# Moving the preparation of attention biases to an earlier stage, and their loads to another DMA queue

## The chip, the cores and the metric

One core of a Trainium2 chip runs the whole program: two transformer blocks, one after the other, in one launch. The metric is device time in microseconds (us), lower is better, for one execution; three executions of the kernel before are at hand, and one further execution was recorded by the hardware profiler.

## The reference, cut to what matters

The first block has two layers, A and B, the second has two more. Each layer is a mixer (attention) and then a feed-forward part. What the change touches is the second layer's attention over a grid of 8 rows and 64 columns of tokens, which adds a learned bias for every relative position, and the keys and values of 256 memory tokens, which each of the two layers attends to as well:

```python
def first_block(x, mem, ...):
    mem_n = rmsnorm(mem, norm_mem)
    for i in range(DEPTH):                       # DEPTH = 2: layer A, layer B
        h = rmsnorm(x, norm_mix[i])
        mkv = mem_n @ w_mem_kv[i]                # keys and values of the 256 memory tokens
        if i % 2 == 0:
            q, k, v, qm = split(h @ w_in_a[li])
            y_tok = windowed_gqa(q, k, v, sink_a[li])
        else:
            q, k, v, qm = split(h @ w_in_b[li])
            y_tok = neighbourhood_attn(q, k, v, rpb_b[li])
        y_mem = memory_attn(qm, mk, mv)
        x = x + concat([y_tok, y_mem]) @ w_out[i]
        h = rmsnorm(x, norm_ffn[i])
        gu = h @ w_gate_up[i]                    # 1024 -> 2 * 2816
        x = x + (silu(gu[..., :D_FF]) * gu[..., D_FF:]) @ w_down[i]

def neighbourhood_attn(q, k, v, rpb):            # rpb: 12 heads x 15 x 31
    bias = rpb[:, dr_idx][:, :, :, dc_idx]       # row and column offset of query and key
    s = einsum(q, k) * D ** -0.5 + bias
    ...
```

## The kernel before, in words

**Arithmetic.** Every float32 product is made of three matmuls: a number is split into a high part `hi` (ScalarE, ACT, L429) and the rest `lo` (VectorE, DVE, L430), and `mm3` (L254 to L256; `linN`, L283 to L285, with the operands the other way round) adds hi by hi, hi by lo and lo by hi in PSUM. A weight piece (`wpiece`) is a 128x4x256 tile: one DMA on SyncE's queue (SP, L213) into one of four `raw` buffers, then the split into one of four `hi` and `lo` buffers. From the fifth feature tile of a feed-forward part on, `seven` (loads at L304) and `blocks_to` make a larger product of seven block products, with additions by DVE and ACT around them.

**Layer A's attention (about 30 to 200 us).** The pairs of heads pass through four-step units: scores (`qk`, L847 and L848), softmax (DVE L721, then exp on ACT, L723), transposes of the probabilities on TensorE (PE, `tr`, L1166) and their copy out of PSUM by ACT (L1168), and the product with the values (`pv`, L1177). Between these units a list of generators, `fill` (L1183), is stepped, so that PE has other work while the softmax runs: query tiles, then `memory_kv()`, then the last query tiles `q_tiles([20, 21, 22, 23])`, then the output projection. `memory_kv` makes keys and values of the memory tokens for both layers: the keys are copied out of PSUM (L872), split and copied to the other half of the partitions (`stack_k`: ACT L834, DVE L835, GpSimd (POOL) L840 and L841), the values are copied out at L880. Layer A's are used at once; layer B's go to a DRAM tile `memd` by five DMAs on SP (L886).

**Layer A's feed-forward part (254 to 573 us).** `ffn` runs 22 tiles f of 128 features, in groups of four (one of two); each tile ends with `put`, whose product at L1043 occurs once for each f. The down projection of one group is spread over the next group's tiles. The same function runs layer B's feed-forward part (831 to 1142 us).

**The biases.** `load_biases` is a generator that `ffn` steps with `next(mid)` at the start of each tile from f = 4 on (L999; `MID = 4`), in layer A alone. It clears a DRAM tile `rpbs` (memset on POOL, one DMA), writes the table into it by eight DMAs on POOL's queue (L1220), spreads it into a second DRAM tile `TBd` by 16 DMAs on SP (L1224; each moves 768 pieces of 128 bytes), and then loads `TBd` into six SBUF tiles `TB` (L1230) and, by `memory_back`, `memd` into five tiles `memb` (L897), all on SP. In layer B, POOL makes the masked biases out of `TB` (L1334 and following), and PE reads `memb` in the memory attention.

**What sets the order.** The program is written through a scheduler: it takes the instructions in the order in which the generators make them, with what each waits for, and by its own model of durations lays down one order for each engine and each queue; the chip then executes every engine's list in that order, and waits for semaphores where something isn't ready. So a generator's place in `fill` is a wish, and what an engine really executes is its list.

## Time and profile before

| what | value |
|---|---|
| time, three executions | 2470.08, 2470.57 (median), 2476.79 us |
| profiled execution: its own time | 2472.3 us |
| profiled execution: span | 2470.6 us |
| mean granted clock of PE, share of full | 0.995 |
| PE busy | 2428.9 us (98%) |
| DVE, ACT, POOL busy | 1812.7, 1185.9, 232.4 us |
| layer A's feed-forward part, first to last L1043 | 254.2 to 572.6 us |
| layer B's feed-forward part, first to last L1043 | 831.4 to 1142.1 us |

The span is what the profiler saw from the first to the last instruction; the execution's own time is 1.7 us longer and is the one to hold against the three times. PE is busy nearly all the time, so a change in time shows as PE idle time that comes or goes, or as a stretch in which PE's granted clock (PEclk, in shares of 2.4 GHz) is lower. A busy time on another engine matters only where PE waits for it.

### The profile page before, as it was taken

What the parts mean: (1) busy time and instruction counts of PE and PEld (TensorE: products, weight loads), DVE (VectorE), ACT (ScalarE), POOL (GpSimd) and SP (SyncE); (2) the same over time, 40 slices, a digit from 0 to 9 for tenths busy, and PEclk for the clock granted to TensorE, in tenths of its full rate; (3) what the DMA queues carried; (4) which work ended last, traced back from release to release, by engine and by line L of the source; (5) the groups of instructions that cost most, each with busy time, mean ns of one, the idle gap of its engine ahead of it and who ended that gap; (6) DMA issues with size and microseconds to landing.
All of it is one profiled execution on the core that took longest, in us unless ns stands there. A gap on an engine that the chain in (4) does not pass through costs nothing.

```text
span 2470.6 us, 44131 instructions
## 1 busy us (share of the span) xinstructions
PE 2428.9 (98%) x17446; PEld 2195.4 (89%) x17446; DVE 1812.7 (73%) x3531; ACT 1185.9 (48%) x2175; POOL 232.4 (9%) x359
## 2 busy tenths in 40 slices
PE   7999999999999999999999999999999999999999
PEld 6787789998887889998989999899999988989998
DVE  6875767777775778777766656888886775788885
ACT  4764435444565445445432233445444664445543
POOL 3120300003130100001011110200000000200000
PEclk9999999999999999999999999999999999999999
DMA  6152234444222223333411123123334222223332
GB/s 189 52 141 82 77 83 113 116 145 145 86 74 78 77 86 107 103 102 101 130 44 52 35 83 91 56 86 107 98 95 142 58 57 75 69 83 109 99 98 82
DMA packets 345443, 229.17 MB, mean 93 GB/s; under 512 B 54435, under 2 KB 335444, under 8 KB 345236
## 3 DMA queue, kind: packets, MB, share of 16 engines
q1 hardware_dynamic: 342212, 217.55, 30.0%
q0 software_dynamic: 2864, 8.77, 1.2%
q8 instruction: 137, 2.24, 0.4%
q14 instruction: 70, 0.57, 0.1%
q10 hardware_dynamic: 160, 0.04, 0.0%
HBM read 214.10 MB, written 13.74 MB: 92 GB/s over the span
## 4 chain that ended last, share of the span: by engine, by line
PE 83%; DVE 10%; issue 3%; ACT 2%; POOL 1%; SPq 1%; DMA 1%; DVEq 0%; ACTq 0%; POOLq 0%
PE mm L254 19%; PE mm L256 19%; PE mm L255 19%; PE pss L254 3%; PE pss L256 3%; PE pss L255 3%; DVE lo L430 2%; PE pso L254 1%; PE pso L256 1%; PE pso L255 1%; PE pss L847 1%; DVE xb L430 1%; PE pso L808 1%; PE pss L848 1%; PE pso L2045 1%
## 5 line engine op out<-in xcount | busy, mean ns | idle before, releaser
L429 ACT ACTIVATE hi<-raw 128x1024 fp32r<-128x1024 f32 (+1 forms) x454 | 470.7, 1039 | 520.5 <-PE pss L255 245.5
L430 DVE TENSOR_TENSOR lo<-raw,hi 128x1024 fp32r<-128x1024 f32 (+1 forms) x454 | 550.6, 1215 | 131.7 <-ACT hi L429 130.8
L254 PE MATMUL mm<-xh,hi 128*128 128x264 f32 (+3 forms) x1256 | 413.2, 329 | 8.0 <-ACT xh L508 2.4
L255 PE MATMUL mm<-xl,hi 128*128 128x264 f32 (+3 forms) x1256 | 405.3, 323 | 1.3 <-DVE xl L509 1.2
L256 PE MATMUL mm<-xh,lo 128*128 128x264 f32 (+3 forms) x1256 | 404.6, 323 | 0.0
L254 PE MATMUL mm<-ah,hi 128*128 128x512 f32 (+1 forms) x880 | 308.8, 352 | 7.5 <-DVE ut L404 4.9
L256 PE MATMUL mm<-xb,lo 128*128 128x256 f32 (+2 forms) x1088 | 308.1, 283 | 4.2 <-DVE lo L430 4.2
L255 PE MATMUL mm<-al,hi 128*128 128x512 f32 (+1 forms) x880 | 307.9, 350 | 0.1
L256 PE MATMUL mm<-ah,lo 128*128 128x512 f32 (+1 forms) x880 | 307.7, 350 | 0.0
L254 PE MATMUL mm<-xb,hi 128*128 128x256 f32 (+2 forms) x1088 | 307.3, 282 | 0.0
L255 PE MATMUL mm<-xb,hi 128*128 128x256 f32 (+2 forms) x1088 | 306.9, 282 | 0.0
L254 PEld LDWEIGHTS mm<-xh,hi 128*128 128x128 f32 x1256 | 238.8, 190 | 32.7 <-issue 6.7
L255 PEld LDWEIGHTS mm<-xl,hi 128*128 128x128 f32 x1256 | 238.9, 190 | 18.6 <-DVE xl L509 2.7
L256 PEld LDWEIGHTS mm<-xh,lo 128*128 128x128 f32 x1256 | 238.4, 190 | 18.4 <-issue 0.5
L687 DVE TENSOR_TENSOR xr<-mm,xr 128x512 f32<-128x512 f32 (+1 forms) x288 | 158.1, 558 | 124.1 <-PE mm L256 123.9
L256 PEld LDWEIGHTS mm<-xb,lo 128*128 128x128 f32 x1088 | 205.6, 189 | 5.1 <-DVE lo L430 5.0
L254 PEld LDWEIGHTS mm<-xb,hi 128*128 128x128 f32 x1088 | 205.5, 189 | 3.1 <-ACT hi L429 0.7
L255 PEld LDWEIGHTS mm<-xb,hi 128*128 128x128 f32 x1088 | 205.5, 189 | 2.2
L254 PEld LDWEIGHTS mm<-ah,hi 128*128 128x128 f32 x880 | 165.5, 188 | 29.8 <-DVE ut L404 6.6
L256 PEld LDWEIGHTS mm<-ah,lo 128*128 128x128 f32 x880 | 165.5, 188 | 22.7
L255 PEld LDWEIGHTS mm<-al,hi 128*128 128x128 f32 x880 | 165.5, 188 | 18.9 <-DVE al L430 1.1
L254 PE MATMUL pss<-xb,hi 128*128 128x256 f32 (+2 forms) x544 | 154.6, 284 | 0.0
(526 smaller groups left out, 5041.4 us busy)
## 6 DMA issues: line engine op xcount, KB each, us to landing
raw<-in_w_gate_up_dram SPq DMA_DIRECT2D x142, 256.0 KB, 3.0
raw<-in_ffn_w_up_dram SPq DMA_DIRECT2D x142, 256.0 KB, 3.0
raw<-in_w_down_dram SPq DMA_DIRECT2D x40, 512.0 KB, 3.4
raw<-in_ffn_w_down_dram SPq DMA_DIRECT2D x40, 512.0 KB, 3.4
raw<-in_mix_w_in_dram SPq DMA_DIRECT2D x28, 512.0 KB, 3.8
raw<-in_w_in_b_dram SPq DMA_DIRECT2D x20, 512.0 KB, 3.8
a<-in_w_gate_up_dram SPq DMA_DIRECT2D x34, 256.0 KB, 3.4
a<-in_ffn_w_up_dram SPq DMA_DIRECT2D x34, 256.0 KB, 2.9
```

The costliest lines, as they stand in the source:

```text
L254: PE.matmul(ps, r32(hi), r32(xh), start=first, stop=False, skip_group_check=more)
L255: PE.matmul(ps, r32(hi), r32(xl), start=False, stop=False, skip_group_check=more)
L256: PE.matmul(ps, r32(lo), r32(xh), start=False, stop=last, skip_group_check=more)
L429: A.activation(r32(dst_h), src, AF.Copy)
L430: V.tensor_tensor(r32(dst_l), src, dst_h, ALU.subtract)
L687: V.tensor_tensor(X[j][:, o:o + n], ps[:, :n], X[j][:, o:o + n], ALU.add)
L808: PE.matmul(po[64 * hh:64 * hh + 64, b * P:(b + 1) * P], self.vals(b, j, h), pt[:, (2 * hh + j) * P:(2 * hh + j + 1) * P], start=j == 0, s ...
L847: PE.matmul(ps[:, :n], r32(q), r32(k[0][:, k0:k0 + n]), start=True, stop=False)
L848: PE.matmul(ps[:, :n], r32(q), r32(k[1][:, k0:k0 + n]), start=False, stop=True)
L2045: PE.matmul(po[64 * hh:64 * hh + 64, b * P:(b + 1) * P], vt[b + j][:, kv * 64:kv * 64 + 64], PT[:, (2 * hh + j) * P:(2 * hh + j + 1) * P], ...
```

## The change

The generator `load_biases` is cut in three. `biases_out` (memset, and the nine DMAs on POOL's queue that fill `rpbs`) becomes the first generator of layer A's `fill`. `biases_columns` (the 16 DMAs `TBd<-rpbs`, on SP as before) is called twice there: columns 0 to 7 ahead of `memory_kv()`, columns 8 to 15 behind it and ahead of the last query tiles. `biases_back` (the six loads `TB<-TBd` and the five loads `memb<-memd`) is called once, ahead of the last group's down projection in layer A's `ffn`, and issues on POOL's queue instead of SP's. `ffn` no longer steps a generator per tile. No operation is added or removed otherwise.

```diff
--- before.py
+++ after.py
@@ -890,11 +890,11 @@
             memK.append(kst)
             memV.append(vt)
 
-    def memory_back():
+    def memory_back(eng):
         d = memK[1]
         t = [slot("memb") for _ in range(5)]
         for i, x in enumerate(t):
-            nc.sync.dma_start(x[:, :512], d[i * P:(i + 1) * P, :])
+            eng.dma_start(x[:, :512], d[i * P:(i + 1) * P, :])
         memK[1] = [[(t[2 * i + hh][:, :256], t[2 * i + hh][:, 256:512]) for hh in range(2)] for i in range(2)]
         memV[1] = [t[4][:, :256], t[4][:, 256:512]]
 
@@ -979,7 +979,8 @@
             o = max(lo, d)
             V.scalar_tensor_tensor(out[:, o:T], src[:, o - d:T - d], taps[n - 1 - d], out[:, o:T], ALU.mult, ALU.add)
 
-    def ffn(X, T, nj, wgu, wd, taps, done, lo=0, mid=None):
+    def ffn(X, T, nj, wgu, wd, taps, done, mid=None, lo=0):
+
 
         xs = nj.xs
         lg = max(0, lo - 2)
@@ -996,8 +997,6 @@
 
         def up(f, put, between):
             c = f * P
-            if mid is not None and f >= MID:
-                next(mid, None)
             gt, ut = wk("gt"), wk("ut")
             if f < NPLAIN:
                 pcs = [wcols(wgu, 4 * h, [(c, P), (DFF + c, P)]) for h in range(2)]
@@ -1055,6 +1054,8 @@
                 up(f0 + i, put, more)
                 more(8)
             before = down(gi, acts)
+        if mid is not None:
+            mid()
         run(before)
 
     def dump(X, T, off=0):
@@ -1078,6 +1079,31 @@
     mnat = load_rows_of(a["mem"][0], NMEM)
 
 
+    TB, rel = [], {}
+
+    def scap(off, dims):
+        return bass.AP(tensor=rel["sc"].tensor, offset=rel["sc"].offset + off, ap=dims)
+
+    def biases_out():
+
+        rel["sc"] = dp.tile([P, 288], F32, name="rpbs")
+        z = slot("zpad")[:, :288]
+        G.memset(z, 0.0)
+        G.dma_start(rel["sc"], z)
+        for r in range(8):
+            G.dma_start(scap(r * 4608 + 8, [[384, 12], [48, 8], [1, 31]]), a["rpb_b"][0, :, 7 - r:15 - r, :])
+        yield 0.1
+
+    def biases_columns(lo, hi):
+
+        if lo == 0:
+            rel["td"] = dp.tile([P, 6 * 512], F32, name="TBd")
+        for cc in range(lo, hi):
+            nc.sync.dma_start(rel["td"][8 * cc:8 * cc + 8, :].rearrange("p (i j) -> p i j", j=32),
+                              scap(15 - cc, [[4608, 8], [48, 96], [1, 32]]))
+        yield 0.1
+
+
     def layer_a(X):
         w = a["w_in_a"][0]
         sk = cp.tile([P, 24], F32, name="sinkA")
@@ -1180,8 +1206,8 @@
 
         order = [0, 1, 3, 4, 2, 5, 6, 7]
         heads = A_PAIRS + [(12, 13), (14, 15)]
-        fill = Fill(q_tiles([6, 9, 7, 10], [3, 4]), q_tiles([2, 5, 8, 11], [2, 5]), memory_kv(),
-                    q_tiles([20, 21, 22, 23], [6, 7]))
+        fill = Fill(biases_out(), q_tiles([6, 9, 7, 10], [3, 4]), q_tiles([2, 5, 8, 11], [2, 5]),
+                    biases_columns(0, 8), memory_kv(), biases_columns(8, 16), q_tiles([20, 21, 22, 23], [6, 7]))
         wo = a["w_out"][0]
         return mixer(lambda p: PairA(p) if p < 6 else MemPair(0, p - 6, qt[p]), order,
                      lambda p: fill.until(lambda: p in qt and (p < 6 or len(memV) == 2)), fill,
@@ -1204,35 +1230,15 @@
                         X[j][:, :S].rearrange("p (r c) -> p r c", c=64), ALU.add)
         lag.put(XB[j])
 
-    TB = []
-
-    def load_biases():
-
-        sc = dp.tile([P, 288], F32, name="rpbs")
-        z = slot("zpad")[:, :288]
-        G.memset(z, 0.0)
-        G.dma_start(sc, z)
-
-        def scap(off, dims):
-            return bass.AP(tensor=sc.tensor, offset=sc.offset + off, ap=dims)
-
-        for r in range(8):
-            G.dma_start(scap(r * 4608 + 8, [[384, 12], [48, 8], [1, 31]]), a["rpb_b"][0, :, 7 - r:15 - r, :])
-
-        td = dp.tile([P, 6 * 512], F32, name="TBd")
-        for cc in range(16):
-            nc.sync.dma_start(td[8 * cc:8 * cc + 8, :].rearrange("p (i j) -> p i j", j=32),
-                              scap(15 - cc, [[4608, 8], [48, 96], [1, 32]]))
-            if cc > 1:
-                yield
+    def biases_back():
         for hp in range(6):
             TB.append(slot("TB"))
-            nc.sync.dma_start(TB[hp][:, :512], td[:, hp * 512:(hp + 1) * 512])
-        memory_back()
+            G.dma_start(TB[hp][:, :512], rel["td"][:, hp * 512:(hp + 1) * 512])
+        memory_back(G)
 
     nb = Norm(S, ("norm_mix", 1), "rsB")
     lag = Lag(nb, NLAG)
-    ffn(X, S, nf, a["w_gate_up"][0], a["w_down"][0], None, to_cols, mid=load_biases())
+    ffn(X, S, nf, a["w_gate_up"][0], a["w_down"][0], None, to_cols, biases_back)
     lag.end()
     if stop == "a":
         return dump(XB, S)
@@ -1863,7 +1869,7 @@
     def ffn2(X, li, done, lo=0):
         fw = load_rows([([("f", li, j) for j in range(3)],
                          a["ffn_conv_w_2"][li].rearrange("j (c p) -> (j c) p", p=P), NFF)], f"fwcol{li}")
-        ffn(X, T, nf, a["ffn_w_up_2"][li], a["ffn_w_down_2"][li], lambda f: tap(fw, ("f", li), 3, f), done, lo)
+        ffn(X, T, nf, a["ffn_w_up_2"][li], a["ffn_w_down_2"][li], lambda f: tap(fw, ("f", li), 3, f), done, None, lo)
 
     def to_norm(j, out):
         resid(X)(j, out)
@@ -2173,7 +2179,6 @@
 LATER = (0, 3)
 ABQ = 16
 POOLSQ = (1, 3, 5, 7)
-MID = 4
 MSTEP = 2
 RATIO_A = 0.7
 RATIO_B = 1.2
```

The three places where this changes an engine's list, as the scheduler laid it down (names with a number are buffers; x4 means four like instructions; line numbers are those of the kernel that the fence is of).

SP's queue in layer A's attention, the kernel before: the last two loads for the memory keys and values, the two loads of the last query weights (`raw<-in_w_in_a`), loads of the output weights, and the first store to `memd`.

```order
L213 DMA raw_1740<-in_w_mem_kv_dram 128x4x256
L213 DMA raw_1746<-in_w_mem_kv_dram 128x4x256
L213 DMA raw_1810<-in_w_in_a_dram 128x4x256
L213 DMA raw_1816<-in_w_in_a_dram 128x4x256
L213 DMA raw_2009<-in_w_out_dram 64x2x256 x4
L213 DMA raw_2164<-in_w_out_dram 64x256 x2
L213 DMA raw_2164<-in_w_out_dram 64x2x256
L213 DMA raw_2164<-in_w_out_dram 64x256
L213 DMA raw_2164<-in_w_out_dram 64x3x256
L213 DMA raw_2363<-in_w_out_dram 64x2x256
L886 DMA memd<-memk_1694 128x512
L213 DMA raw_2363<-in_w_out_dram 64x2x256 x2
```

The same place in the changed kernel:

```order
L213 DMA raw_1761<-in_w_mem_kv_dram 128x4x256
L213 DMA raw_1767<-in_w_mem_kv_dram 128x4x256
L1102 DMA TBd<-rpbs 768x32
L886 DMA memd<-memk_1715 128x512
L886 DMA memd<-memk_1716 128x512
L886 DMA memd<-memk_1751 128x512
L886 DMA memd<-memk_1752 128x512
L886 DMA memd<-memv_1676 128x512
L1102 DMA TBd<-rpbs 768x32 x7
L213 DMA raw_1839<-in_w_in_a_dram 128x4x256
L213 DMA raw_1845<-in_w_in_a_dram 128x4x256
L213 DMA raw_2038<-in_w_out_dram 64x2x256 x4
```

The two loads of query weights stood ahead of all five stores to `memd`; now they stand behind them, and behind eight `TBd<-rpbs` DMAs (one ahead of the stores, seven behind).

PE in layer A's attention, the kernel before, within the memory keys of layer B (L254 to L256 with `xm` are the keys' matmuls, L847 and L848 attention scores):

```order
L254 MATMUL mm_1704<-xm_1251,hi_1658 128x256
L255 MATMUL mm_1704<-xm_1251,hi_1658 128x256
L847 MATMUL pss_1573<-kh_362,qs_1136 128x384
L848 MATMUL pss_1573<-kl_363,qs_1136 128x384
L256 MATMUL mm_1704<-xm_1251,lo_1659 128x256
L254 MATMUL mm_1704<-xm_1261,hi_1664 128x256
L255 MATMUL mm_1704<-xm_1261,hi_1664 128x256
L256 MATMUL mm_1704<-xm_1261,lo_1665 128x256
L254 MATMUL mm_1704<-xm_1272,hi_1664 128x256
L255 MATMUL mm_1704<-xm_1272,hi_1664 128x256
```

The changed kernel, just ahead of those keys (L1203 is `pv`, L1192 the transposes `tr`); behind these rows come 48 matmuls for layer B's keys, 48 for its values and 48 for the last two query tiles, with no attention row between them:

```order
L1203 MATMUL pso_1989<-PT_1894,vA_233 64x128
L1192 MATMUL pss_1934<-ident,Pa_1370 128x128 x3
L1203 MATMUL pso_1989<-PT_1901,vA_233 64x128
L1203 MATMUL pso_1989<-PT_1894,vA_234 64x128
L1203 MATMUL pso_1989<-PT_1901,vA_234 64x128
L1203 MATMUL pso_1989<-PT_1894,vA_235 64x128
L1203 MATMUL pso_1989<-PT_1901,vA_235 64x128
L1192 MATMUL pss_1941<-ident,Pa_1376 128x128 x3
L1203 MATMUL pso_1989<-PT_1938,vA_234 64x128
L1203 MATMUL pso_1989<-PT_1945,vA_234 64x128
L1203 MATMUL pso_1989<-PT_1938,vA_235 64x128
L1203 MATMUL pso_1989<-PT_1945,vA_235 64x128
```

The attention steps that were spread among the keys' and values' matmuls now stand together ahead of them, one unit's transposes close behind another's products.

SP's queue in layer A's feed-forward part at f = 4 to 6, the kernel before (L304 and L213 load weights):

```order
L304 DMA raw_3417<-in_w_gate_up_dram 128x4x128
L304 DMA raw_3415<-in_w_gate_up_dram 128x4x128
L1224 DMA TBd<-rpbs 768x32 x5
L304 DMA raw_3416<-in_w_gate_up_dram 128x4x128
L213 DMA raw_3514<-in_w_down_dram 128x2x256
L1224 DMA TBd<-rpbs 768x32
L304 DMA raw_3573<-in_w_gate_up_dram 128x4x128
L304 DMA raw_3571<-in_w_gate_up_dram 128x4x128
L304 DMA raw_3572<-in_w_gate_up_dram 128x4x128
L213 DMA raw_3670<-in_w_down_dram 128x2x256
```

The changed kernel at the same place:

```order
L304 DMA raw_3428<-in_w_gate_up_dram 128x4x128
L304 DMA raw_3426<-in_w_gate_up_dram 128x4x128
L304 DMA a_3739<-in_w_gate_up_dram 128x4x128
L304 DMA raw_3427<-in_w_gate_up_dram 128x4x128
L213 DMA raw_3525<-in_w_down_dram 128x2x256
L304 DMA raw_3583<-in_w_gate_up_dram 128x4x128
L304 DMA raw_3581<-in_w_gate_up_dram 128x4x128
L304 DMA raw_3582<-in_w_gate_up_dram 128x4x128
L304 DMA a_3894<-in_w_gate_up_dram 128x4x128
```

The list now holds weight loads alone. The eleven loads of `TB` and `memb`, which stood in it at f = 18, are in POOL's list behind that part's last arithmetic on POOL. The lists of PE, DVE and ACT for layer A's feed-forward part are now row for row those of layer B's.

## Rows read from the trace of the kernel before

**Rows 1.** The page: the span, then busy us, share and count of each engine.

```profile
span 2470.6 us, 44131 instructions
...
PE 2428.9 (98%) x17446; PEld 2195.4 (89%) x17446; DVE 1812.7 (73%) x3531; ACT 1185.9 (48%) x2175; POOL 232.4 (9%) x359
```

**Rows 2.** Line L1043, 240 to 600 us: count, ns min/median/max, first and last start.

```profile
L1043 DVE TENSOR_TENSOR ut<-ut,gt x22: 683/685/693, 254.2 to 572.6; 128x512 f32<-128x512 f32 x22
```

**Rows 3.** The same view, 700 to 1300 us: the feed-forward part of layer B.

```profile
L1043 DVE TENSOR_TENSOR ut<-ut,gt x22: 676/684/718, 831.4 to 1142.1; 128x512 f32<-128x512 f32 x22
```

**Rows 4.** Windows: busy us (xcount) of PE, PEld, DVE, ACT, POOL; PEclk, DMA share.

```profile
340.00:345.00 5.00, 3.09 (x16) 2.07 (x15) 4.20 (x8) 3.33 (x6) 0.00 (x0) 1.00 0.00 0
346.70:350.20 3.50, 3.50 (x19) 3.50 (x18) 1.90 (x3) 1.00 (x2) 0.00 (x0) 0.51 0.85 235
885.00:1000.00 115.00, 115.00 (x822) 107.55 (x821) 88.29 (x127) 54.29 (x85) 0.00 (x0) 1.00 0.34 100
```

**Rows 5.** Timeline of SP in layer A's feed-forward part: start us, us, instruction.

```profile
307.45 3.74 SPq L1224 DMA_DIRECT2D TBd<-rpbs  x5
```

**Rows 6.** Timeline of ACT there; in brackets its idle time before and who ended it.

```profile
318.34 1.06 ACT L429 ACTIVATE hi<-raw 128x1024 fp32r<-128x1024 f32 x1 [3.75 <-DMA TBd<-rpbs]
```

**Rows 7.** Timeline of SP late in that feed-forward part.

```profile
509.62 2.87 SPq L1230 DMA_DIRECT2D TB<-TBd  x6
512.59 3.47 SPq L897 DMA_DIRECT2D memb<-memd  x5
```

**Rows 8.** Tile TBd, whole program: DMA issues (ns), and us from issue to landing.

```profile
L1224 SPq DMA_DIRECT2D TBd<-rpbs x16: 475/507/908, 307.5 to 464.7; - x16
...
DMA to landing us min/median/max: 2.8/3.1/3.6
```

**Rows 9.** Timeline of SP in layer A's attention.

```profile
128.08 2.98 SPq L213 DMA_DIRECT2D raw<-in_w_in_a_dram  x2
...
156.70 0.39 SPq L886 DMA_DIRECT2D memd<-memv  x1
```

**Rows 10.** Windows there, columns as in rows 4.

```profile
130.00:140.00 10.00, 10.00 (x80) 9.45 (x80) 9.05 (x28) 7.96 (x22) 4.16 (x6) 1.00 0.29 90
```

**Rows 11.** Timeline of PE, end of the second memory values, first query tile.

```profile
152.89 0.28 PE L285 MATMUL mm<-lo,xm 128*128 128x256 f32 x1
153.01 0.39 PE L254 MATMUL mm<-xh,hi 128*128 128x512 f32 x1
153.24 0.40 PE L255 MATMUL mm<-xl,hi 128*128 128x512 f32 x1
```

**Rows 12.** Line L880, the memory values' copies out of PSUM.

```profile
L880 DVE TENSOR_SCALAR memv<-mm,memrs x4: 469/472/476, 147.1 to 154.4; 128x256 f32<-128x256 f32 x4
```

**Rows 13.** DMA issues from 60 to 80 us: KB each, median us to landing.

```profile
raw<-in_w_mem_kv_dram SPq DMA_DIRECT2D x3, 512.0 KB, 3.4
```

**Rows 14.** Tile hi from 128 to 160 us: the split of weights.

```profile
L430 DVE TENSOR_TENSOR lo<-raw,hi x8: 1205/1218/1308, 126.8 to 154.8; 128x1024 fp32r<-128x1024 f32 x8
L429 ACT ACTIVATE hi<-raw x7: 1039/1060/1062, 128.4 to 153.1; 128x1024 fp32r<-128x1024 f32 x7
```

**Rows 15.** Lines L1168 and L723 from 100 to 170 us: attention's work on ACT.

```profile
L1168 ACT COPY PT<-pss x25: 354/461/484, 100.7 to 169.7; 128x384 f32<-128x384 f32 x13, 128x256 f32<-128x256 f32 x12
...
L723 ACT ACTIVATE Pa<-Pa,negm x22: 497/598/623, 102.7 to 165.9; 128x384 f32<-128x384 f32 x12, 128x256 f32<-128x256 f32 x10
```

**Rows 16.** A window between the layers, columns as in rows 4.

```profile
1346.80:1357.00 10.20, 10.20 (x69) 9.20 (x67) 3.94 (x9) 1.74 (x4) 0.00 (x0) 0.50 0.33 104
```

**Rows 17.** Timeline of POOL from 290 to 620 us.

```profile
580.38 0.85 POOL L1252 CAST xeh<-xh 128x64 fp32r<-128x64 f32 x1 [275.53 <-ACT xh L508]
...
601.70 0.45 POOL L1334 TENSOR_SCALAR_AFFINE_SELECT be<-TB 128x256 f32<-128x256 f32 x1
```

**Rows 18.** Tile xr, DMAs issued from POOL, and us to landing.

```profile
L700 POOL DMA_DIRECT2D xr<-xd x32: 538/538/873, 164.5 to 2037.1; - x32
...
DMA to landing us min/median/max: 2.8/4.1/10.9
```

## The prediction, made before the changed kernel was run

> **What bounds the kernel now.** I read the page first: PE is busy for 2428.9 of 2470.6 us [rows 1], so the question is where PE waits or runs at a lower clock, in the two stages that the change touches. The profiled execution took 2472.3 us by its own time; the median of the runs is 1.7 us less.
>
> For the feed-forward part of layer A there is a control in the same trace: layer B's runs the same function without the biases. Read the first and last start of the product that ends each tile. Layer A's go from 254.2 to 572.6, which is 318.4 us [rows 2]; layer B's from 831.4 to 1142.1, which is 310.7 us [rows 3]. So 7.7 us are lost in layer A. The windows show them as holes in PE (3.09 busy of 5 us at 340 to 345) and a stretch of 3.5 us at 0.51 of the clock, the 1.2 GHz level, just behind that hole; layer B's part has 115 us without either [rows 4]. The two timelines show the likely start: five `TBd` DMAs hold SP's queue for 3.74 us between weight loads [rows 5], and then ACT stands 3.75 us before it can split a piece, released by a `TBd` DMA [rows 6]. From there ACT and DVE are late by several pieces, which PE feels one tile later.
>
> In layer A's attention PE is busy for all of 130 to 140 us [rows 10]: no slack that a gain could hide in, and any wait there is a loss.
>
> **The change part by part.** *(1) No `TBd` DMAs in the feed-forward part.* Its lists become those of layer B's part, so I take layer B's time: **-7.7 us**. The least is 0, if the hole at 340 us has another cause; more than 7.7 has no row for it.
>
> *(2) The loads of `TB` and `memb` on POOL.* SP is freed of 2.87 + 3.47 us of issue at 509.62 [rows 7], but no loss is found there: 0. POOL does nothing between the biases' DMAs and 580.38, and the first `TB` is read at 601.70 [rows 17]. The loads wait for buffers that the last tiles free, at the latest behind the product at 572.6 [rows 2]; a DMA issued from POOL holds it 538 ns and lands within 10.9 us at the longest [rows 18]. Three late issues end at about 574.2 and land by 585.1, so 0 here too; behind the work that covers them stand 16 us.
>
> *(3) The table into `rpbs`, at the start of attention:* nine DMAs on POOL, 9 x 0.54 = 4.9 us by the row of another POOL DMA [rows 18], ahead of the second pair's distance biases. I take 0, because POOL makes each pair's biases while PE is still at the pair before; if they come late all the same, the worst is 4.9 us, once.
>
> *(4) The last query weights behind `memd` and eight `TBd` DMAs.* This is the largest term. Before, they were issued at 128.08, the last `memd` store at 156.70 [rows 9], and PE went from the last value matmul at 152.89 straight to the query tile at 153.01 [rows 11]. Now SP's list holds them behind the last `memd` store, which needs the values, and behind seven more `TBd`. PE's list has nothing between the values and these query tiles, so it must stand. From the last value matmul on: its own end 0.28 [rows 11], the copy out of PSUM 0.47 [rows 12], the store's issue 0.39 [rows 9], that is 1.1; seven `TBd` issues at the median of 0.507 [rows 8], 3.6; the load to its landing 3.4 [rows 13]; the split's high part 1.06 [rows 14]. That is 9.2 us to the first query matmul. The third one waits for the low part, 1.22 [rows 14], of which two matmuls at 0.23 [rows 11] cover 0.46: 0.8 more, 10.0. Ends: 9.8 with the shortest issue (0.475). The longest: in the trace of before the last store came 3.8 us behind the last value matmul (156.70 - 152.89), not 0.8, because POOL's copies of the keys were late; and five `TBd` took 3.74, so seven take 5.2. That gives 10.0 + 3.0 + 1.6 = 14.6. With less ACT work beside it than before, the copies should be nearly in time; I take half of each surplus of issue and a quarter of the copies', about **+11.5 us**.
>
> The page "DMA: Bandwidth & Descriptors" of the Trainium skill says, in its section "Why small descriptors are slow (HBM only)", that every packet carries a fixed overhead, so that small ones waste the engines' time; by it the load behind seven `TBd` of 128-byte pieces would land late as well. The sum above has the load at its undisturbed 3.4; the trace's `TBd` DMAs land in 2.8 to 3.6 us [rows 8], so none of them outlasts the next one's issue by much.
>
> *(5) Attention steps without other work.* Ahead of layer B's memory keys, attention stands in PE's list without fill between. Each copy of transposed values takes 0.46 us and each exp 0.60 [rows 15], and PE has only a few 0.12-us matmuls to put behind them. Four copies and two exps laid bare make 3.0 us; nothing laid bare makes 0. The list puts `pv` right behind the transposes it needs, which is nearest to bare: **+3.0 us**.
>
> *(6) The clock.* Behind the 1.9 us hole at 340 us PE ran 3.5 us at half clock [rows 4], which costs half of that, 1.7 us; another such stretch lasted 10.2 us [rows 16], 5.1. A wait of 11 us is longer than the first hole, so I take the first price: **+1.7 us**; 0 to 5.1.
>
> The sum on the profiled execution: 2472.3 - 7.7 + 11.5 + 3.0 + 1.7 = 2480.8; less 1.7 to stand with the median, **2479.0 us**.
>
> **The rivals.** *The short wait.* The copies are in time, attention covers itself and the clock stays up: (4) at 9.8, (5) and (6) at 0. Then 2470.6 - 7.7 + 9.8 = 2472.7, no change that can be measured. For it: POOL's and ACT's idle time grows once attention is out of the way. Against it: three terms must all be at their low end.
>
> *The wait is not on PE's path.* Slower turns into faster if the last query weights reach PE in time all the same, for instance if the values of layer B end while attention or fill still has work for PE. The point from which it decides is a wait of 7.7 us in all. With none, 2470.6 - 7.7 = 2462.9. Against it stand the two lists: SP's puts the weights behind the values, PE's puts nothing between.
>
> *The feed-forward part keeps its hole.* At 340 us no DMA is in flight (share 0.00) [rows 4], and it may be a chain of ACT and DVE that would be late without `TBd` too. Then 2479.0 + 7.7 = 2486.7. Against it: layer B's part, and the 3.75 us in which ACT waits for `TBd` [rows 6].
>
> *The clock stays low for long.* A half-clock stretch as in [rows 16] behind the new wait costs 5.1 instead of 1.7: 2482.4. The page "TensorE: Matmul & The Clock Gate" of the Trainium skill, in "HAM oscillation — how this bites in real kernels", says that each wait for a DMA that lets the clock fall is paid for again by work at half rate. The trace agrees with it at 346.7 us [rows 4], where the price was the 1.7 us of (6).
>
> **How the numbers follow.** Within 0.3% (7.4 us) a measurement of this kernel can't tell a time from no change; that is 2463.2 to 2478.0 around the median. Chances: the forecast 0.45, the short wait 0.27, the low clock 0.08, the hole that stays 0.10, the wait off the path 0.08, `TB` or `rpbs` in the way after all 0.02. The forecast's own terms reach from -7.7 + 9.8 to -7.7 + 14.6 + 3.0 + 5.1, that is 2472.7 to 2485.6; about a quarter of it lies below 2478.0. So slower 0.34 + 0.08 + 0.10 + 0.02 = 0.54, within 0.11 + 0.27 = 0.38, faster 0.08. The range leaves out the rival on the faster side and half of the highest one: 2469 to 2487.
>
> **What would show it.** Right: L1043's first and last start 310.7 us apart in layer A too, no half clock near 347; between 140 and 175 us one PE wait of 9 to 15 us for the split of `w_in_a`, with SP standing at `memd` and then issuing seven `TBd` ahead of the two loads; a stretch at half clock behind it; `TB` landed by 586. Wrong: PE without a wait of over 7 us there, or a first query matmul within 3 us of the last value matmul; or holes in the feed-forward part with no `TBd` in it.

## The result, and the profile after

The changed kernel takes 2487.24 us (median of 6 runs, 2482.65 to 2492.93), the kernel before 2472.61 us beside it: a ratio of 1.0061, 95% interval 1.0045 to 1.0077. It is slower by 14.6 us, where the forecast had 8.4 (2479.0 against a median of 2470.6 from three executions); the range ended at 2487.0. Single runs of one kernel spread over some 10 us here (one source is shown in the last section); so below, differences of medians stand beside what a trace shows for one stage.

The page of the changed kernel: 18.4 us more span than before [rows 1], and PE is busy 4.2 us longer for the same 17446 matmuls.

```profile
span 2489.0 us, 44128 instructions
...
PE 2433.1 (98%) x17446; PEld 2198.2 (88%) x17446; DVE 1812.3 (73%) x3531; ACT 1189.4 (48%) x2175; POOL 233.1 (9%) x370
```

**Attention.** The forecast wait is there. SP's timeline (start, us, what) has the last `memd` store, then seven `TBd` DMAs, then the last query weights:

```profile
156.54 3.07 SPq L886 DMA_DIRECT2D memd<-memk  x4
162.41 0.32 SPq L886 DMA_DIRECT2D memd<-memv  x1
162.78 4.97 SPq L1102 DMA_DIRECT2D TBd<-rpbs  x7
167.80 1.19 SPq L213 DMA_DIRECT2D raw<-in_w_in_a_dram  x2
```

ACT and PE in the same stretch; in brackets how long each had stood, and who released it:

```profile
172.87 1.06 ACT L429 ACTIVATE hi<-raw 128x1024 fp32r<-128x1024 f32 x1 [15.36 <-DMA raw<-in_w_in_a_dram]
```

```profile
161.58 0.28 PE L285 MATMUL mm<-lo,xm 128*128 128x256 f32 x1
173.98 0.79 PE L254 MATMUL mm<-xh,hi 128*128 128x512 f32 x1 [12.12 <-ACT hi L429]
```

PE stood 12.12 us between the last value matmul and the first query matmul, which followed each other in 0.12 us before [rows 11]. The windows (columns as in [rows 4]) show the stretch ahead of the wait, the wait itself and the first query matmuls:

```profile
140.00:150.00 10.00, 8.46 (x76) 5.99 (x70) 3.43 (x9) 6.47 (x15) 1.80 (x4) 1.00 0.00 0
150.00:160.00 10.00, 9.48 (x80) 9.33 (x79) 7.12 (x11) 3.87 (x7) 3.86 (x8) 1.00 0.18 68
161.90:174.00 12.10, 0.02 (x1) 0.03 (x1) 0.53 (x2) 1.06 (x1) 0.00 (x0) 0.60 0.85 180
174.00:178.00 4.00, 3.96 (x9) 2.67 (x10) 1.98 (x2) 1.06 (x1) 0.00 (x0) 0.51 0.93 168
```

PE was at half clock (0.51) for the first 4 us behind the wait. From 140 to 160 us it is idle for 1.5 and 0.5 us, where before it was busy all the time. In PE's timeline 1.3 us of that are waits for ACT's copies of the transposed probabilities, in the attention steps without fill; 0.7 are waits for the split of the weights for layer B's keys, 0.52 of it in one place (150.67).

**Layer A's feed-forward part** ran from 271.7 to 587.8 us, 316.1 us, against 318.4 before [rows 2] and 310.7 in layer B's [rows 3]:

```profile
L1042 DVE TENSOR_TENSOR ut<-ut,gt x22: 683/685/691, 271.7 to 587.8; 128x512 f32<-128x512 f32 x22
```

Product by product, the trace is within 0.5 us of layer B's part up to f = 17; at f = 18 it is some 5.4 us late and stays so. There the loads on POOL begin (POOL's and SP's timelines):

```profile
519.29 3.21 POOL L1236 DMA_DIRECT2D TB<-TBd  x6 [204.23 <-PE mm L256]
522.49 1.07 POOL L897 DMA_DIRECT2D memb<-memd  x2
```

```profile
513.75 8.50 SPq L304 DMA_DIRECT2D raw<-in_w_gate_up_dram  x3
```

SP's last load of those three goes out at 521.9, among eight loads of 256 KB from POOL (the other three go out from 574.8 on). DVE's timeline shows who was to read it, the view of its tile how long two weight loads there took to land, and the windows what PE lost:

```profile
524.35 0.69 DVE L308 TENSOR_TENSOR raw<-raw,raw 128x512 f32<-128x512 f32 x1
530.26 0.69 DVE L309 TENSOR_TENSOR raw<-raw 128x512 f32<-128x512 f32 x1 [5.22 <-DMA raw<-in_w_gate_up_dram]
```

```profile
DMA to landing us min/median/max: 4.3/6.3/8.3
```

```profile
525.00:530.00 5.00, 3.86 (x31) 3.43 (x30) 0.04 (x1) 1.93 (x4) 0.00 (x0) 1.00 0.87 297
530.00:533.00 3.00, 0.86 (x4) 0.73 (x5) 2.74 (x4) 0.00 (x0) 0.00 (x0) 0.99 0.02 5
533.00:536.30 3.30, 3.30 (x10) 2.62 (x9) 1.04 (x3) 0.00 (x0) 0.00 (x0) 0.50 0.74 233
```

L309 stands right behind L308 in DVE's list and waits 5.22 us for the load; PE is idle for 3.3 of 8 us and then at half clock for 3.3.

So 17.5 us are lost ahead of the part (271.7 against 254.2) and 2.4 gained in it. The other 3.3 us of the span come behind it, where the lists are those of before but for a few steps next to the part's end; one stretch at half clock that the trace of before doesn't have (3.4 us at 2051.9) is 1.7 of them.

### The profile page after: what moved, and what is told of

It is laid out like the page before. It is cut to its first block, busy times and chain, and to the rows that moved or that the text cites. A ratio compares the mean times of both kernels' runs of the same rounds, so it can differ in the third digit from the quotient of the medians.

```text
span 2489.0 us, 44128 instructions
## 1 busy us (share of the span) xinstructions
PE 2433.1 (98%) x17446; PEld 2198.2 (88%) x17446; DVE 1812.3 (73%) x3531; ACT 1189.4 (48%) x2175; POOL 233.1 (9%) x370
## 4 chain that ended last, share of the span: by engine, by line
PE 62%; DVE 7%; issue 2%; ACT 1%; POOL 1%; POOLq 0%; ACTq 0%; DVEq 0%
PE mm L254 14%; PE mm L255 14%; PE mm L256 14%; PE pss L254 2%; PE pss L256 2%; PE pss L255 2%; DVE lo L430 1%; PE pso L256 1%; PE pso L255 1%; PE pso L254 1%; DVE xb L430 1%; PE pso L808 1%; PE pso L2051 1%; PE pss L847 1%; PE pss L1624 1%
## 5 line engine op out<-in xcount | busy, mean ns | idle before, releaser
L254 PE MATMUL mm<-xh,hi 128*128 128x264 f32 (+3 forms) x1256 | 414.1, 330 | 20.5 <-ACT hi L429 12.1
L256 PE MATMUL mm<-xh,lo 128*128 128x264 f32 (+3 forms) x1256 | 405.5, 324 | 0.0
L254 PE MATMUL mm<-ah,hi 128*128 128x512 f32 (+1 forms) x880 | 308.9, 352 | 8.2 <-DVE ut L404 5.0
L256 PE MATMUL mm<-ah,lo 128*128 128x512 f32 (+1 forms) x880 | 308.2, 350 | 3.3 <-DVE lo L430 3.3
L256 PE MATMUL mm<-xb,lo 128*128 128x256 f32 (+2 forms) x1088 | 307.5, 283 | 0.0
L254 PE MATMUL mm<-xb,hi 128*128 128x256 f32 (+2 forms) x1088 | 307.1, 282 | 0.0
L254 PEld LDWEIGHTS mm<-xh,hi 128*128 128x128 f32 x1256 | 239.2, 190 | 45.2 <-ACT hi L429 12.3
L256 PEld LDWEIGHTS mm<-xh,lo 128*128 128x128 f32 x1256 | 239.1, 191 | 18.9 <-DVE lo L430 0.8
L254 PEld LDWEIGHTS mm<-xb,hi 128*128 128x128 f32 x1088 | 205.7, 189 | 2.5 <-ACT ut L400 0.2
L256 PEld LDWEIGHTS mm<-xb,lo 128*128 128x128 f32 x1088 | 205.3, 189 | 0.0
L254 PEld LDWEIGHTS mm<-ah,hi 128*128 128x128 f32 x880 | 165.6, 188 | 31.1 <-DVE ut L404 6.7
L256 PEld LDWEIGHTS mm<-ah,lo 128*128 128x128 f32 x880 | 165.7, 188 | 26.0 <-DVE lo L430 3.7
L254 PE MATMUL pss<-xb,hi 128*128 128x256 f32 (+2 forms) x544 | 154.6, 284 | 0.3 <-DVE ut L395 0.3
```

The costliest lines, as they stand in the source:

```text
L254: PE.matmul(ps, r32(hi), r32(xh), start=first, stop=False, skip_group_check=more)
L256: PE.matmul(ps, r32(lo), r32(xh), start=False, stop=last, skip_group_check=more)
```

## The experiments

The theory from these traces: the change has two separate faults. (a) Eight `TBd` DMAs and the `memd` stores stand ahead of the last query weights in SP's list. (b) The loads on POOL make a weight load late which the lists expect in time. Without either, the forecast gain in the feed-forward part is there. Every run was timed beside the kernel before; "part" is the time from the first to the last product in layer A's feed-forward part.

### Only fault (a) taken away: all columns ahead of the memory keys

```diff
-                    biases_columns(0, 8), memory_kv(), biases_columns(8, 16), q_tiles([20, 21, 22, 23], [6, 7]))
+                    biases_columns(0, 16), memory_kv(), q_tiles([20, 21, 22, 23], [6, 7]))
```

> Edit: the changed kernel, with all 16 TBd DMAs ahead of memory_kv (none between memory_kv and the last query tiles); the loads of TB and memb stay on POOL's queue. SP's list then holds the last query weights ahead of the memd stores again. Theory (the wait of PE for the query weights, about 12 us with the half-clock stretch behind it, and the attention left without fill are one fault of the list; the loads on POOL are a second one of about 5 us): attention gives back about 16, so 2472.6 - 7.4 + 5 = about 2470 us, no PE wait over 2 us for the split of w_in_a, still a wait of about 5 us of DVE for a weight load near f = 18. Rival (the order of attention itself is the loss, the queue only took what would have been lost elsewhere): over 2480 us.

Measured: 2475.29 us, ratio 1.0009 (0.9997 to 1.0020); 12 us less than the change. SP's list has the query weights ahead of the stores again, and the part begins at 256.2 instead of 271.7:

```profile
68.43 11.83 SPq L1102 DMA_DIRECT2D TBd<-rpbs  x16
80.37 27.61 SPq L213 DMA_DIRECT2D raw<-in_w_mem_kv_dram  x4
149.26 1.50 SPq L213 DMA_DIRECT2D raw<-in_w_in_a_dram  x2
...
162.63 0.54 SPq L886 DMA_DIRECT2D memd<-memv  x1
```

```profile
L1042 DVE TENSOR_TENSOR ut<-ut,gt x22: 682/685/692, 256.2 to 569.4; 128x512 f32<-128x512 f32 x22
```

The wait was fault (a), and the rival falls. 2 us remain in attention (256.2 against 254.2), in a hole from 140 to 150 us:

```profile
140.00:150.00 10.00, 8.23 (x68) 5.87 (x68) 4.80 (x10) 7.12 (x15) 1.79 (x4) 1.00 0.00 0
```

The late weight load near f = 18 is still there (DVE waits 4.5 us; the part takes 313.2, 2.8 more than the same kernel with the loads on SP, below). It costs half of what it cost in the changed kernel: PE is idle for 2.6 us around it, and keeps its full clock afterwards:

```profile
517.00:525.00 8.00, 8.00 (x54) 7.34 (x53) 5.58 (x9) 3.99 (x7) 0.00 (x0) 1.00 0.38 118
```

The median is 5 us above the 2470 expected. The trace doesn't say why: it is of the shortest of the 12 executions (2464.26 us), with PE at 0.999 of its clock on the mean.

### Only fault (b) taken away: the loads on SP at f = 18

```diff
-        if mid is not None:
-            mid()
         run(before)
...
+            if mid is not None and f == 18:
+                mid()
...
-            G.dma_start(TB[hp][:, :512], rel["td"][:, hp * 512:(hp + 1) * 512])
-        memory_back(G)
+            nc.sync.dma_start(TB[hp][:, :512], rel["td"][:, hp * 512:(hp + 1) * 512])
+        memory_back(nc.sync)
```

> Edit: the changed kernel, with the loads of TB and memb on SP's queue at f = 18, as in the kernel before; the 16 TBd DMAs stay where the change put them. Theory (the loads on POOL run beside a weight load that SP issues, which lands 5 us late; on SP they stand in one line with the weight loads, which come in time): the feed-forward part takes 310.7 us from first to last product, about 5 us less than with the change, so 2487.2 - 5 = about 2482 us. Rival (the loads cost the same from either queue, since they move the same 2.8 MB through the same DMA engines at the same tile): 316 us for that part, 2487 us.

Measured: 2482.25 us, ratio 1.0039 (1.0027 to 1.0051), 5.0 below the change (9.4 above the kernel before, where the change was 14.6 above it); the part takes 310.5 us:

```profile
L1044 DVE TENSOR_TENSOR ut<-ut,gt x22: 681/684/691, 271.3 to 581.8; 128x512 f32<-128x512 f32 x22
```

The same 2.8 MB cost no time on SP. The timelines of SP and DVE say why: the third weight load now stands behind the eleven loads in SP's line and goes out at 525.80, and DVE's list, laid down with these loads in SP's line, reads it only at 532.04, 6.2 us later, with six other steps between L308 and L309.

```profile
518.86 2.87 SPq L1236 DMA_DIRECT2D TB<-TBd  x6
521.82 3.62 SPq L897 DMA_DIRECT2D memb<-memd  x5
525.80 0.38 SPq L304 DMA_DIRECT2D raw<-in_w_gate_up_dram  x1
```

```profile
523.20 0.68 DVE L308 TENSOR_TENSOR raw<-raw,raw 128x512 f32<-128x512 f32 x1
...
532.04 0.68 DVE L309 TENSOR_TENSOR raw<-raw 128x512 f32<-128x512 f32 x1
```

In the list of the changed kernel the same load had 3.2 us (521.9 to 525.0, where L308 ends). In the kernel before, the three weight loads from 490 to 530 us whose landing the trace tells, none of them issued while the loads of `TB` and `memb` were under way, landed in about that:

```profile
DMA to landing us min/median/max: 2.9/2.9/3.0
```

So the list of the changed kernel leaves this load almost no slack. The loads slow each other down on SP's queue too. In the kernel before, those of `memb` whose landing the trace tells took twice as long:

```profile
DMA to landing us min/median/max: 5.8/5.9/6.0
```

And by the updates of its semaphore in this run's trace the weight load issued at 525.80 landed at 531.3, after 5.5 us, no earlier than in the changed kernel (530.2). What differs is the place of its reader: here the load still lands 0.7 us ahead of it.

### Both taken away

```diff
-                    biases_columns(0, 8), memory_kv(), biases_columns(8, 16), q_tiles([20, 21, 22, 23], [6, 7]))
+                    biases_columns(0, 16), memory_kv(), q_tiles([20, 21, 22, 23], [6, 7]))
...
+            if mid is not None and f == 18:
+                mid()
...
-            G.dma_start(TB[hp][:, :512], rel["td"][:, hp * 512:(hp + 1) * 512])
-        memory_back(G)
+            nc.sync.dma_start(TB[hp][:, :512], rel["td"][:, hp * 512:(hp + 1) * 512])
+        memory_back(nc.sync)
```

> Edit: both of the first two edits: all 16 TBd DMAs ahead of memory_kv, the loads of TB and memb on SP's queue at f = 18. Theory (the change has two faults, and what is left is its gain in the feed-forward part): 2472.6 - 7.7 = about 2465 us, 310.7 us from first to last product, no wait of PE over 2 us in attention for the query weights. Rival (moving the TBd DMAs into attention costs there what it gains in the feed-forward part, wherever they stand): 2472 us or more.

Measured: 2467.81 us, ratio 0.9986 (0.9971 to 1.0001), 5.0 below the kernel before by the medians, though the interval just reaches no change; the part takes 310.4 us and begins at 259.0:

```profile
L1044 DVE TENSOR_TENSOR ut<-ut,gt x22: 682/684/691, 259.0 to 569.4; 128x512 f32<-128x512 f32 x22
```

In the part the gain of the change comes through once its two faults are gone, less what attention still loses. (The part begins at 259.0; in the first run, with the same lists up to there, it began at 256.2. This trace has PE at 0.66 of its clock on the mean from 10 to 30 us, that one at 1.00.) Against the first run, timed beside it, this one also shows fault (b) alone: 7.5 us less by the medians, 2.8 by the traces of the part.

### The loads on POOL in the kernel before, and at another place

```diff
-            nc.sync.dma_start(TB[hp][:, :512], td[:, hp * 512:(hp + 1) * 512])
+            G.dma_start(TB[hp][:, :512], td[:, hp * 512:(hp + 1) * 512])
...
-            nc.sync.dma_start(x[:, :512], d[i * P:(i + 1) * P, :])
+            G.dma_start(x[:, :512], d[i * P:(i + 1) * P, :])
```

> Edit: the kernel before, with the loads of TB and memb on POOL's queue instead of SP's; all else as before. Theory (loads on POOL aren't held back by SP's line, so a weight load that SP issues within some 8 us of them lands late): a late weight load near f = 16 to 18, 2472.6 + 5 = about 2477 us; if no weight load with a reader waiting falls into those 8 us, nothing, 2472.6. Rival (the loss near f = 18 in the changed kernel has nothing to do with the queue): 2472.6 us with weight loads landing in about 3 us beside the loads.

Measured: 2472.72 us, ratio 0.9999 (0.9987 to 1.0010). The loads began at 467.75, and weight loads beside them took up to 9.7 us to land, but no reader was due, and the part took 318.4 us as before; DVE waited 0.2 us once (timelines of POOL, SP and DVE, and the landings).

```profile
467.75 3.27 POOL L1230 DMA_DIRECT2D TB<-TBd  x6 [163.59 <-DMA TBd<-rpbs]
```

```profile
DMA to landing us min/median/max: 4.3/7.0/9.7
```

```profile
473.12 0.37 SPq L304 DMA_DIRECT2D raw<-in_w_gate_up_dram  x1
```

```profile
481.27 0.68 DVE L306 TENSOR_TENSOR raw<-raw,a 128x512 f32<-128x512 f32 x1
```

The load issued at 473.12 was read 8.2 us later, by L306, which waits for its semaphore. (The 0.2 us are L307's wait at 482.15, for a load issued at 477.50.)

So I expected that an earlier place would be free in the changed kernel as well. It keeps its loads on POOL and only asks for them at f = 18:

```diff
-        if mid is not None:
-            mid()
         run(before)
...
+            if mid is not None and f == 18:
+                mid()
```

> Edit: the changed kernel, with the loads of TB and memb still on POOL's queue, but asked for at f = 18 instead of ahead of the last down projection, which gives them buffers that come free earlier; the TBd DMAs stay where the change put them. Theory (a load on POOL costs time only if a weight load that an engine is about to read is issued beside it; in the run of the kernel before with loads on POOL they went at 467.8 us, weight loads took up to 9.7 us to land, and nobody was waiting): the first loads go near 477 us, weight loads beside them land in 5 to 10 us, the part takes 310.5 to 312 us, about 2482 us like the run with the loads on SP. Rival (loads on POOL cost 5 us in the changed kernel at any place in this part): 316 us for the part, 2487 us.

Measured: 2487.03 us, ratio 1.0060 (1.0042 to 1.0077). The rival holds, with 4.5 us instead of its 5: the loads began at 456.15, DVE waited 4.8 us for L309's weights at f = 14, the part took 315.0 us (waits of DVE: us in total, times, longest).

```profile
DVE raw L309 <- DMA raw<-in_w_gate_up_dram: 5.9, 4, 4.8
```

It isn't the tile that matters but the list. The kernel before with the loads on POOL, whose SP line still holds `TBd` DMAs, left 8.2 us between that load and its reader; the changed kernel's lists left 3.0 here (458.74 to 461.7, where L308 ends) and 3.2 at f = 18. That refines theory (b). That it is the `TBd` DMAs which make the lists wider there is likely, but no run takes them out alone.

### The table earlier, and columns one at a time

What in the kernel before costs 7.8 us: any `TBd` between weight loads, or the burst of five that waited for its table? Its trace first shows what doesn't. The 3.75 us that ACT stands at 318.34 [rows 6], 64.1 us behind the part's first product, were read as a wait for a `TBd` DMA. At the same place of layer B's part, where there is no such DMA, ACT stands as long, released by PE:

```profile
895.50 1.06 ACT L429 ACTIVATE hi<-raw 128x1024 fp32r<-128x1024 f32 x1 [3.73 <-PE pss L255]
```

What layer B's part doesn't have is this wait one tile later, for a copy that stands ahead of weight splits in ACT's list (there that copy waits 1.0 us at the longest):

```profile
329.53 0.37 ACT L387 COPY u<-mm 128x256 f32<-128x256 f32 x1 [7.61 <-PE mm L256]
```

So what costs time seems to be the order of the lists that were laid down around the burst. First, the table four tiles earlier and the columns two tiles earlier, attention untouched:

```diff
-            if mid is not None and f >= MID:
+            if mid is not None:
...
+        yield
+        yield
         for cc in range(16):
...
-            if cc > 1:
-                yield
+            yield
```

> Edit: the kernel before, with its biases generator stepped from f = 0 on instead of f = 4: the table goes into rpbs at f = 0, three TBd DMAs stand in one place of SP's list near f = 2, and one per tile after that; TB and memb on SP at f = 18, as before; attention is untouched. Theory (the 7.8 us lost in layer A's feed-forward part of the kernel before come from the burst of five TBd DMAs that wait for a table which is only just being written; one TBd per tile, ready when its turn comes, costs nothing): first product at 254.2 as before, 310.4 to 312 us for the part, about 2466 to 2468 us. Rival (any TBd between weight loads makes a later weight load late, as loads on POOL do): 314 us or more for the part, 2470 us or more.

Measured: 2468.27 us, ratio 0.9978 (0.9967 to 0.9989). The part takes 312.5 us, a little over the range of the theory and under that of the rival, and begins at 254.6: single `TBd` DMAs cost at most 2 us, the burst cost the rest, and the longest wait at L387 is 1.9 us. Three columns still stand together here, but ahead of the part (250.6 to 251.9) and with their table long written; whether the burst's size or its wait for the table did the harm, this run doesn't separate.

Then the changed kernel's early table, one column per tile from f = 2 on, and the loads on SP at f = 18; the scheduler put twelve columns ahead of the part, six of them by 131 us, singly or in pairs among the weight loads:

```diff
-                    biases_columns(0, 8), memory_kv(), biases_columns(8, 16), q_tiles([20, 21, 22, 23], [6, 7]))
+                    memory_kv(), q_tiles([20, 21, 22, 23], [6, 7]))
...
+            if mid is not None and f > 1:
+                mid(f)
...
+    def biases_back(f):
+        if f < 18:
+            next(biases_columns(f - 2, f - 1))
+        if f != 18:
+            return
```

> Edit: the changed kernel, with the TBd DMAs asked for one per tile of the feed-forward part from f = 2 on (the scheduler moves six of them up into attention, in ones and twos between weight loads, and the others to the start of the feed-forward part), and the loads of TB and memb on SP at f = 18. Theory (what costs in attention is a group of TBd DMAs ahead of the memory weights or the query weights, through the order that the scheduler lays down): at most 2 us in attention, first product at 254 to 256, 310.4 to 312 us for the part, about 2466 to 2469 us. Rival (single TBd DMAs between weight loads cost too): first product past 258 or more than 314 us for the part, over 2470 us.

Measured: 2460.71 us, ratio 0.9948 (0.9932 to 0.9964). It beats both kernels. Attention takes as long as before, though its lists are not quite those of before, and the part takes 309.7 us, 8.8 less than in the kernel before:

```profile
L1044 DVE TENSOR_TENSOR ut<-ut,gt x22: 683/685/693, 254.1 to 563.8; 128x512 f32<-128x512 f32 x22
```

The same kernel, timed again as the partner of the next run:

> Edit: none against the run with one column per tile; it is timed again as the partner of the next run. Theory: first product at 254 to 256, 309.5 to 311 us for the feed-forward part, 2459 to 2465 us again. Rival (its 2460.7 us was luck of the clock): 2466 us or more, the kernel before less the 8.8 us of its trace and not more.

Measured: 2463.93 us, ratio 0.9962 (0.9947 to 0.9977); the part takes 310.0 us. The two medians are 13.7 and 8.4 us below the kernel before; the second, of 12 executions against 6, is what the trace of the part accounts for, and the rest of the first is best taken as luck.

### Fault (b) put back into the best version

```diff
-            nc.sync.dma_start(TB[hp][:, :512], rel["td"][:, hp * 512:(hp + 1) * 512])
-        memory_back(nc.sync)
+            G.dma_start(TB[hp][:, :512], rel["td"][:, hp * 512:(hp + 1) * 512])
+        memory_back(G)
```

and the call ahead of the last down projection, as in the change.

> Edit: the kernel with one column per tile, with the loads of TB and memb put back on POOL's queue ahead of the last down projection, as the change has them. Theory (the lists laid down without these loads in SP's line leave no slack for a weight load that lands late beside them): DVE waits 4 to 6 us once near f = 17 for a weight load, the part takes 313 to 315 us, 3 to 6 us above the partner run. Rival (the waits in the changed kernel needed what came before them, such as the wait in attention): no such wait, the time of the partner run.

Measured: 2468.25 us, 4.3 above its partner, timed beside it (ratio to the kernel before 0.9986, 0.9975 to 0.9998, against 0.9962). The wait is back without fault (a) and without a loss in attention, and the part takes 315.8 us, 5.8 more than its partner's:

```profile
506.31 0.69 DVE L308 TENSOR_TENSOR raw<-raw,raw 128x512 f32<-128x512 f32 x1
512.37 0.69 DVE L309 TENSOR_TENSOR raw<-raw 128x512 f32<-128x512 f32 x1 [5.37 <-DMA raw<-in_w_gate_up_dram]
```

### The columns on POOL's queue (a miss)

The 2 us in attention that the first run left: do they come from the columns in SP's list? The kernel with both faults away, its `TBd` DMAs issued from POOL:

```diff
-            nc.sync.dma_start(rel["td"][8 * cc:8 * cc + 8, :].rearrange("p (i j) -> p i j", j=32),
+            G.dma_start(rel["td"][8 * cc:8 * cc + 8, :].rearrange("p (i j) -> p i j", j=32),
```

> Edit: as the run with columns early and loads on SP, but the 16 TBd DMAs are issued on POOL's queue, so that SP's list in attention holds weight loads and memd stores alone, in the order of the kernel before. Theory (what is left of the loss in attention, about 2 us of PE idle time from 140 to 150 us, comes from the TBd DMAs in SP's list, behind which the scheduler put the memory weights and so took the fill away from attention): the first product of the feed-forward part starts within 1 us of the kernel before (254.2 in its trace), 310.4 us for the part, 2472.8 - 7.8 = about 2465 us. Rival (the 2 us come from the distance biases, which POOL makes later behind the rpbs DMAs): POOL is busier still, so 2 us or more remain, about 2468 or more.

Measured: 2471.84 us, ratio 0.9995 (0.9982 to 1.0008); the part begins at 258.3, 4 us late. SP's list was that of the kernel before and the hole at 140 us is gone (PE busy for 9.98 us from 140 to 150), but there are new ones from 90 to 130:

```profile
90.00:110.00 20.00, 18.97 (x131) 13.07 (x130) 14.01 (x39) 13.65 (x37) 10.31 (x14) 1.00 0.50 118
110.00:120.00 10.00, 8.80 (x65) 6.15 (x65) 7.56 (x23) 9.01 (x27) 2.33 (x2) 1.00 0.00 1
120.00:130.00 10.00, 8.20 (x58) 6.40 (x57) 7.32 (x26) 6.28 (x18) 0.00 (x0) 1.00 0.01 2
```

```profile
122.39 0.45 PE L847 MATMUL pss<-kh,qs 128*128 128x384 f32 x1 [1.45 <-DVE negm L721]
```

```profile
92.06 9.20 POOL L1102 DMA_DIRECT2D TBd<-rpbs  x13
113.62 2.41 POOL L1169 TENSOR_SCALAR ab<-dist 128x384 f32<-128x384 f32 x2 [12.37 <-DVE es L730]
```

PE waits there for the softmax (`negm`), here and once at 105.60, 2.4 of the 4.0 us that it is idle. The rival's reason isn't seen: POOL's 13 DMAs end at 101.3, and the next biases then wait 12.4 us for DVE (`es`, L730), not for POOL. So the theory is wrong, for the loss stays with SP's list as before, and the rival has its time without its reason. In the runs with the columns in a group, PE's list for attention differs more from that of the kernel before than with one column per tile, and 2 to 4 us go there; that the list is the reason is a guess, and what in the scheduler does that was not tried.

## Why the prediction was wrong

The sign and the main term were right; one step was wrong, the price of the loads on POOL, put at 0. Whether the median lies 0.2 us outside the range or inside it is luck, with single runs 10 us apart. The forecast stood on a median of 2470.6 us from three executions, where six gave 2472.6. What failed is in the change itself: 14.6 us instead of 8.4, and most of the 6.2 between them is step (2).

- **(1) No `TBd` in the feed-forward part, -7.7.** Right: up to f = 17 the part ran as layer B's, and with the loads on SP the whole of it took 310.5 us. The rival that the hole stays fell. But ACT's 3.75 us [rows 6], which were held against it, are no wait for `TBd`: layer B's part has them too.
- **(2) The loads on POOL, 0. This step failed.** It looked at when the loads were ready for their own readers, with 16 us to spare, and at SP's freed time. It did not ask what the loads would do to transfers beside them, or when they would go out: eight went out from 519.29 on, 68 us ahead of the last product (587.8 here), which it took as the latest point, and while the part's weights were still being loaded. It gave "`TB` or `rpbs` in the way after all" a chance of 0.02. By the medians the loads cost +5.0 (change against the run with loads on SP), +7.5 (with the columns early) and +4.3 (put back into the best version); by the traces of the part 5.6, 2.8 and 5.8. They did so through one weight load that landed in 8.3 instead of 2.9 us, a DVE wait of 5.2 us and, in the dearer cases, a half-clock stretch. The page "DMA: Bandwidth & Descriptors" of the Trainium skill says, in "Issuing engines are not separate DMA queues", that DMAs of all engines run on the same 16 DMA engines and interleave. The trace agrees: 8.3 us beside POOL's loads. Leaving SP's line took away no transfer; it took away the 6.2 us that the lists otherwise leave between that weight load and its reader.
- **(3) The table at the start of attention, 0.** Right: with the table at that place and the columns one by one the part begins at 254.1, as before.
- **(4) The query weights, +11.5.** Measured 12.12, so the short wait and the wait off PE's path fell. Its parts differ: POOL's copies were in time (no surplus there), but seven `TBd` took 4.97 us of issue, not 3.6, and the load behind them landed in 5.0, not 3.4. The 0.8 for the low part doesn't show as a wait: at half clock the two matmuls ahead took 1.26 us (173.98 to 175.24) and covered it. The sum kept the load at 3.4 because no `TBd` DMA seemed to outlast the next one's issue by much; but with 0.5 us of issue and 2.8 to 3.6 to the landing [rows 8] several are under way at once, so that reading was wrong. The page "DMA: Bandwidth & Descriptors" of the Trainium skill says in "Why small descriptors are slow (HBM only)" that every packet costs a fixed overhead. The trace's 1.6 us fit that, but loads of the output weights went out 1.2 us behind the query weights (169.03), and no run separates the two.
- **(5) Attention without fill, +3.0.** 2.0 us of PE idle time from 140 to 160, of which 1.3 are the laid-bare copies that the term is about and 0.7 the late split of the weights for layer B's keys.
- **(6) The clock, +1.7.** Right in size: behind the wait nine matmuls took 4.0 us, for which 2.1 are enough at 0.23 each, so 1.9. The rival of a clock that stays low for long fell. The hole ahead of 346.7 us [rows 4], which gave the price, ended with a wait for DVE's split (1.94 us at 345.78), not for a DMA.

Terms (4) to (6) come to 16.0, the forecast's 16.2; the part begins 17.5 us late in that trace. Of the other 1.5 us, 0.7 are there by 114 us: the trace has PE at 0.66 of its clock on the mean from 10 to 30 us, where the trace of before has 1.00. The last 0.8 stay open. With (2) at 5, the sum on the median would have been 2484, 3 us below the result, and 2.0 of these 3 come from the median that it stood on; the run without fault (b), 2482.25, is 9.4 above the kernel before where the forecast gave 8.4.

## What to carry to other kernels

Where a scheduler lays down the lists, bulk loads on another engine's queue are only as free as the readers of the loads beside them are late. Here the weight load landed late with the bulk loads on either queue; with them in its own line the lists had put its reader behind the landing. So look up how much time each list leaves between a load's issue and its reader (here 3.2 us against a landing of 2.9 undisturbed and 8.3 beside the bulk) before moving 2.8 MB to a second queue. A group of small DMAs did more harm here than the same DMAs singly, in an in-order line where everything behind the group moves together; spread them one by one, after their source is ready. And when a step is taken off one path, ask of each transfer in it not only whether it comes in time, but whom it makes late.

## What the runs showed of the hardware

Stretches at half clock (1.2 GHz) come and go between executions here, also where the lists are the same and PE is busy all the time. At the place where the kernel before ran 10.2 us at 0.50 [rows 16], the run with early columns, whose list there is the same, shows none:

```profile
1340.00:1350.00 10.00, 10.00 (x125) 8.96 (x124) 6.95 (x19) 2.62 (x5) 0.00 (x0) 1.00 0.13 36
1350.00:1360.00 10.00, 10.00 (x131) 8.97 (x128) 5.07 (x19) 2.46 (x7) 0.00 (x0) 1.00 0.24 73
```

That is 5 us between two executions, as much as fault (b) cost, so single traces were compared stage by stage and kernels by medians. In the changed kernel PE's clock also stayed low for about 4 us after work came back behind the long wait (12.12 us), and for 3.3 us behind the late weight load; behind the late weight load of the run with all columns early it did not fall at all.
